# Cached value pages in even and odd partitions, with the score matmuls reading their keys in the same order

## The chip, the cores and the metric

The kernel runs on one core of one Trainium2 chip. The metric is the device time of one execution in microseconds (us), as the median of several runs. Beside it stands one execution taken by the hardware profiler, whose page and trace are read below.

## What is computed

One inference step of a hybrid decoder layer, for a prompt of 256 tokens and for eight sample sequences of eight new tokens each. The layer adds to its input, one after the other, a mixer (block attention beside a state-space scan), a cross-attention to a memory, and a squared-ReLU MLP. The change touches only the sample sequences' attention to their cached past of 1024 keys, which lie in eight pages of 128 keys; a page table names the pages. In the reference:

```
k_past = cache_k[l][page_table].reshape(bs, -1, ATT_HEADS, HEAD_DIM)
v_past = cache_v[l][page_table].reshape(bs, -1, ATT_HEADS, HEAD_DIM)
...
s = jnp.einsum('bhqd,bhqnkd->bhqnk', qq, kg)
s = jnp.where(mask, s, -jnp.inf).reshape(b, h, qc, n_sel * BLOCK)
p = jax.nn.softmax(s, axis=-1).reshape(b, h, qc, n_sel, BLOCK)
return jnp.einsum('bhqnk,bhqnkd->bhqd', p, vg)
```

A block is 256 keys, so two pages. Three of the four past blocks are attended to, chosen by the product of the query with the mean of the block's keys. Within a block the sum over keys, the maximum and the mean do not depend on the order of the keys, as long as scores and values have the same one.

## The kernel before

All weights are loaded in chunks of 128x1024 (512 KB, tile `wr`), each split by ScalarE and VectorE into a high and a low part (`wh` at L394, `wl` at L395). Each product of activations with weights is then three matmuls of type fp32r (L400, L401, L402). Attention works in plain f32, for which each matmul of the program stands in the trace as two instructions.

The order of TensorE's work is written out by hand as a string of letters, one for each piece of a stream; the letter `S` is the sample attention. The orders of ScalarE, VectorE, GpSimd and of the DMAs are lists of numbers. The change leaves all of them as they are.

`sample_attn(bp)` handles sequences 2bp and 2bp+1, for bp from 0 to 3. For each of the four blocks `n` it fetches, with `pages`, one tile `kv` of shape [128, 2, 512] for each sequence `e`: two pages, 256 KB each, by one DMA each on SyncE's queue (L841). Thirteen buffers of this size are shared by all that uses the name `kv`.

- Keys (`ckT`): a page is stored transposed, so that a partition is a component of the heads and the 512 columns are four groups of 128 keys. The score matmul (L882) takes as its moving operand `kbs[e][:, :, 128*c : 128*c+128]`, that is 128 neighbouring columns of the first page and then 128 of the second, 256 in all. Its stationary operand is the 32 columns of `qs`. Four such matmuls, for two sequences `e` and two groups of heads `g`, write four strips of 32 partitions of the PSUM tile `sc`. Each is done for s = 0 and 1.
- VectorE takes sums and maxima over the 256 columns (L885, L886), ScalarE the exponentials (L908), and TensorE transposes the result in pieces of 128 columns (L921), so that a piece's column becomes a partition of `pT`.
- Values (`cv`): partition k of page q holds the 512 values of key k in `t[:, q, :]`, a row of 2 KB. The value matmul (L936) for q = 0 contracts the first piece of 128 with the first page, that for q = 1 the second piece with the second page.

So a row of a `cv` transfer is 2 KB, and column 128*q + k of the scores is key k of page q.

Of the kernel before, what the change touches and what calls it, by code (L numbers as in the profile page):

```python
# [16 lines left out]
P = 128  # L17
# [105 lines left out]
def _constants():  # L123
    c = np.zeros((P, NCST), np.float32)
    i = np.arange(P)

    def put(name, a):
        lo, hi = CST[name]
        c[:, lo:hi] = a

    put("ident", np.eye(P))
    put("tri", i[:, None] <= i[None, :])
    put("gt", i[:, None] > i[None, :])
    diag = np.where(i[None, :] <= i[:, None], 0.0, NEG)
    put("cmask", np.concatenate([diag, np.zeros((P, P)), diag], axis=1))
    bq, tq = i // 64, i % 8

    om = np.full((P, 14, TS), NEG)
    for b in range(2):
        for t in range(TS):  # L140
            om[(bq == b) & (t <= tq), 6 + b, t] = 0.0
    put("omask", om.reshape(P, 112))
    s = np.arange(64)
    same = s[:, None] // TS == s[None, :] // TS
    a = np.zeros((P, 64))
    a[:64] = same & (s[:, None] <= s[None, :])
    put("tri_s", a)
    a = np.zeros((P, 64))
    a[:64] = same & (s[:, None] > s[None, :])
    put("gt_s", np.concatenate([a, a], axis=1))  # L150
    a = np.zeros((P, NB))
    a[:64] = s[:, None] // TS == np.arange(NB)[None, :]
    put("bmask", a)

    r = i // 32
    put("bquad", np.stack([i % 64 // TS == 4 * (r % 2) + 2 * e + r // 2 for e in range(2)], axis=1))
    put("selq", i[:, None] // 32 == np.arange(32)[None, :])
    put("sel0", np.arange(32)[None, :] == 0)
    put("sel4", np.arange(32)[None, :] == 4)
    put("idx", np.arange(1, 5)[None, :])  # L160
    put("ones", 1.0)
    half = np.float32(10000.0) ** (-np.arange(32, dtype=np.float32) / np.float32(32))
    pos = np.concatenate([np.arange(TP), np.tile(1024 + np.arange(TS), NB)]).astype(np.float32)
    ang = (pos[None, :] * half[:, None]).astype(np.float32)
    cos, sin = np.cos(ang), np.sin(ang)
    r = np.concatenate([np.tile(cos, (4, 1)), np.tile(sin, (4, 1))], axis=1)
    return c, r.astype(np.float32)
# [6 lines left out]
def _rows(w):  # L174

    k, m = w.shape
    return w.reshape(k // P, P, m // P, P).transpose(2, 1, 0, 3)


def _layout(a):  # L180
    f = {k: np.asarray(v) for k, v in a.items()}
    tok = np.concatenate([f["x_prompt"].reshape(TP, 1024), f["x_sample"].reshape(NB * TS, 1024)])
    o = {}
    o["xT"] = tok.T.reshape(8, P, T).transpose(1, 0, 2)
    o["memT"] = f["mem_prompt"].reshape(256, 1024).T.reshape(8, P, 256).transpose(1, 0, 2)
    wi = f["w_in"][0]

    def two(w):

        return _rows(w).reshape(4, 2, P, 512).transpose(0, 2, 1, 3)  # L190
    parts = [
        _rows(wi[:, HALF]), _rows(wi[:, 512 + HALF]), _rows(wi[:, 2048:3072]),
        wi[:, 1024:1536].reshape(4, 2, P, 512).transpose(0, 2, 1, 3), _rows(wi[:, 1536:2048]),
        two(f["w_out"][0][:512]), two(f["w_out"][0][512:]), _rows(f["wk_x"][0]), _rows(f["wq_x"][0]),
        f["wv_x"][0].reshape(4, 2, P, 512).transpose(0, 2, 1, 3),
        two(f["wo_x"][0]),
        _rows(f["w_up"][0]),
        _rows(f["w_down"][0]).reshape(8, P, 4, 1024).transpose(0, 2, 1, 3),
    ]
    o["w"] = np.concatenate([p.reshape(-1, P, 1024) for p in parts])  # L200
    npool = f["cache_k"].shape[1]
    o["ckT"] = f["cache_k"][0].reshape(npool, P, 512)[:, :, HALF].transpose(0, 2, 1).reshape(npool, 4, P, P).transpose(0, 2, 1, 3).reshape(npool, P, 512)
    o["cv"] = f["cache_v"][0].reshape(npool, P, 512)
    o["pt"] = f["page_table"].reshape(1, NB * NPAGE)
    o["mk"] = f["cache_mem_k"][0].transpose(0, 3, 2, 1).reshape(NB, P, 1024)
    o["mv"] = f["cache_mem_v"][0].reshape(NB, 2, P, 512).transpose(0, 2, 1, 3).reshape(NB, P, 1024)
    o["h0"] = f["state_ssm"][0].transpose(0, 3, 1, 2).reshape(NB, P, 512)
    o["sc"] = f["state_conv"][0].transpose(2, 0, 1).reshape(8, P, NB, 3).transpose(1, 0, 2, 3).reshape(P, 192)
    p = np.empty((P, NPRM), np.float32)

    def put(name, v):
        lo, hi = PRM[name]
        p[:, lo:hi] = v

    def cols(v):
        return v.reshape(-1, P).T

    put("g_mix", cols(f["ln_mix_g"]))
    put("g_x", cols(f["ln_x_g"]))
    put("g_mem", cols(f["ln_mem_g"]))  # L220
    put("g_mlp", cols(f["ln_mlp_g"]))
    put("g_ssm", cols(f["ssm_norm_g"]))
    put("conv_w", f["conv_w"][0].T.reshape(8, P, 4).transpose(1, 0, 2).reshape(P, 32))
    put("conv_b", cols(f["conv_b"]))
    put("d_skip", cols(np.repeat(f["d_skip"][0], 64)))
    for n, s in (("qg", f["q_norm_g"][0]), ("kg", f["k_norm_g"][0])):
        put(n, np.tile(s.reshape(2, 32), (1, 4)).T)
    put("qxg", f["qx_norm_g"][0][:, None])
    put("kxg", f["kx_norm_g"][0][:, None])
    put("dt_bias", np.broadcast_to(f["dt_bias"], (P, 8)))  # L230
    put("a_log", np.broadcast_to(f["a_log"], (P, 8)))
    put("w_dt", wi[:, 3072:3080].reshape(8, P, 8).transpose(1, 0, 2).reshape(P, 64))
    o["prm"] = p
    o["cst"], o["rot"] = _constants()
    return {k: np.ascontiguousarray(v) for k, v in o.items()}
# [22 lines left out]
def _body(tc, nc, I, O):  # L258
    V, A, G, S, PE = nc.vector, nc.scalar, nc.gpsimd, nc.sync, nc.tensor
# [40 lines left out]
    def ts(n=512):  # L300
        return tl(tp_, [P, n], "ts", bufs=NTS)
# [7 lines left out]
    def kv(shape, dt=F32):  # L309
        return tl(p1, list(shape), "kv", dt, bufs=NKV)  # L310
# [517 lines left out]
    def pages(b):  # L828

        with ExitStack() as st:  # L830
            if last_page:
                st.enter_context(tc.issue_after(last_page[-1]))
            _, idx = nc.values_load_multi_w_load_instructions(
                pt[0:1, NPAGE * b:NPAGE * b + NPAGE], engines=[mybir.EngineType.SP], min_val=0,
                max_val=I["ckT"].shape[0] - 1,
                skip_runtime_bounds_check_because="the page table indexes the pool")

        def get(name, n):
            t = kv([P, 2, 512])
            for q in range(2):  # L840
                d = S.dma_start(t[:, q, :], I[name][bass.ds(idx[2 * n + q], 1)].rearrange("o p c -> p (o c)"))  # L841
                last_page.append(d.ins)
            return t
        return get

    def sample_attn(bp):
# [29 lines left out]
        for n in range(4):  # L876
            kbs = [gets[e]("ckT", n) for e in range(2)]
            for s in range(2):
                for e in range(2):
                    for g in range(2):  # L880
                        r = 64 * e + 32 * g
                        PE.matmul(ps[r:r + 32, 256 * n:256 * n + 256], qs[:, s, g, b0 + e, :],  # L882
                                  kbs[e][:, :, 128 * (2 * g + s):128 * (2 * g + s) + 128], start=s == 0, stop=s == 1)
            if n % 2:
                V.reduce_sum(gs[:, n - 1:n + 1], pv[:, n - 1:n + 1, :], axis=AX.X)  # L885
                V.reduce_max(m5[:, n - 1:n + 1], pv[:, n - 1:n + 1, :], axis=AX.X)  # L886
            if n < 3:
                yield 1.05, PACE
# [41 lines left out]
        for n in range(4):  # L930
            vbs = [gets[e]("cv", n) for e in range(2)]
            for q in range(2):
                for e in range(2):
                    for g in range(2):
                        r = 64 * e + 32 * g
                        PE.matmul(yv[r:r + 32, 0:256], pT[:, 2 * n + q, r:r + 32], vbs[e][:, q, 256 * g:256 * g + 256],  # L936
                                  start=n == 0 and q == 0, stop=first and n == 3 and q == 1)
# [5 lines left out]
        if first:  # L943
# [21 lines left out]
            t = ts(256)  # L965
# [10 lines left out]
        for h in range(2):  # L976
            a = slice(64 * h, 64 * h + 64)
            for c in range(2):

                i0 = tp[a, 128 * c:128 * c + 128].rearrange("p (e g r) -> p g e r", e=2, g=2)[:, :, :, 16 * c + 8 * h:16 * c + 8 * h + 8]  # L980
                o = ay[a, c:4:2, TP + 16 * bp:TP + 16 * bp + 16].rearrange("p g (e t) -> p g e t", e=2)
# [4 lines left out]
    cv = xT  # L986
# [676 lines left out]
    def all_of(name, *gens):  # L1663
# [8 lines left out]
        return [one(g) for g in gens]  # L1672

    att = all_of("att", then(*[sample_attn(bp) for bp in range(4)]), then(prompt_attn(0), prompt_attn(1)))
    crs = all_of("cross", cross_sample(0), cross_prompt(0), cross_sample(1), cross_prompt(1))
    ys = all_of("y", ssd_all(), ssd_rest())
# [100 lines left out]
```

## Time and profile before

| what | value |
|---|---|
| median of 3 runs | 506.55 us (506.18 to 507.35) |
| the profiled execution's own time | 506.26 us |
| its span, first to last instruction | 504.5 us |
| TensorE busy | 497.7 us, 99% of the span |
| VectorE, ScalarE, GpSimd busy | 329.8, 264.2, 18.8 us |
| score matmuls (L882) | 256 instructions, 16.8 us of TensorE |
| value matmuls (L936) | 256 instructions, 15.4 us of TensorE |
| key and value pages | 64 transfers of 256 KB each |
| granted TensorE clock | 0.999 |

The span runs from the first to the last instruction; 1.8 us of the execution's time lie outside it. Busy time of a group is the union of its instructions, which can overlap on TensorE: each matmul is pipelined and its end is modelled. An engine's "idle before" is time in which it had nothing to run, with what ended it. The chain is followed backward from the last instruction to whatever released it.

### The profile page before, as it was taken

The numbers are of one execution on the slowest core, as the hardware profiler recorded it, in microseconds if no ns is written. First come the engines' busy times: TensorE is split into PE (matmuls) and PEld (weight loads), VectorE is DVE, ScalarE is ACT, GpSimd is POOL, SyncE is SP. The second block draws the span as 40 slices with busy tenths as digits, with TensorE's granted clock in tenths as the row PEclk, the third lists the DMA queues.
The fourth block names the chain that finished last, engine by engine and source line by source line (L and its number), as shares of the span: only waits on it lengthen the run. The fifth ranks groups of instructions, "written<-read, shape, count | busy, mean of one in ns | idle before, by whom it ended". The sixth has DMA issues, their size and how long they took to land.

```text
span 504.5 us, 10435 instructions
## 1 busy us (share of the span) xinstructions
PE 497.7 (99%) x3954; PEld 453.0 (90%) x3954; DVE 329.8 (65%) x681; ACT 264.2 (52%) x552; POOL 18.8 (4%) x58
## 2 busy tenths in 40 slices
PE   8999999999999999999999999999999999999997
PEld 5988787878676899998799999999999999999997
DVE  5878899687596898766659576875675443343431
ACT  7634447959766855646566564444455323233230
POOL 2400000130200000000000000000000000000000
PEclk9999999999999999999999999999999999999999
DMA  8999999899899257778903386553654644454530
GB/s 300 332 378 373 338 359 350 312 356 388 296 369 384 84 179 234 281 264 284 338 3 126 126 295 206 167 191 108 246 173 126 182 160 168 139 191 147 159 110 13
DMA packets 45508, 116.53 MB, mean 231 GB/s; under 512 B 5074, under 2 KB 7378, under 8 KB 45458
## 3 DMA queue, kind: packets, MB, share of 16 engines
q1 hardware_dynamic: 39122, 94.12, 54.1%
q10 hardware_dynamic: 6336, 21.75, 12.4%
q8 instruction: 31, 0.51, 0.4%
q14 instruction: 19, 0.16, 0.1%
HBM read 109.71 MB, written 6.14 MB: 230 GB/s over the span
## 4 chain that ended last, share of the span: by engine, by line
PE 94%; ACT 2%; DVE 2%; DMA 1%; issue 0%; SPq 0%; DVEq 0%
PE mm L400 24%; PE mm L401 23%; PE mm L402 23%; PE sc L882 3%; PE as L936 3%; PE ms L378 2%; PE sc L720 2%; PE as L378 1%; DMA wr<-w 1%; PE sc L1556 1%; PE ms L1658 1%; PE as L1580 1%; PE sc L1557 1%; PE mm L1630 1%; PE sc L1558 1%; PE as L1604 1%
## 5 line engine op out<-in xcount | busy, mean ns | idle before, releaser
L394 ACT ACTIVATE wh<-wr 128x1024 fp32r<-128x1024 f32 (+1 forms) x115 | 118.6, 1034 | 130.4 <-PE mm L401 104.7
L395 DVE TENSOR_TENSOR wl<-wr,wh 128x1024 fp32r<-128x1024 f32 (+1 forms) x115 | 137.0, 1195 | 74.6 <-ACT wh L394 73.6
L400 PE MATMUL mm<-big,wh 128*128 128x320 f32 x528 | 167.0, 316 | 0.0
L401 PE MATMUL mm<-big,wh 128*128 128x320 f32 x528 | 163.1, 309 | 0.1
L402 PE MATMUL mm<-big,wl 128*128 128x320 f32 x528 | 163.1, 309 | 0.0
L400 PEld LDWEIGHTS mm<-big,wh 128*128 128x128 f32 x528 | 99.1, 188 | 8.4 <-issue 6.0
L401 PEld LDWEIGHTS mm<-big,wh 128*128 128x128 f32 x528 | 99.2, 188 | 0.8 <-DVE big L1290 0.3
L402 PEld LDWEIGHTS mm<-big,wl 128*128 128x128 f32 x528 | 99.1, 188 | 0.0
L402 PE MATMUL mm<-hh,wl 128*128 128x320 f32 x256 | 78.9, 308 | 0.0
L401 PE MATMUL mm<-hl,wh 128*128 128x320 f32 x256 | 78.9, 308 | 0.0
L400 PE MATMUL mm<-hh,wh 128*128 128x320 f32 x256 | 78.9, 308 | 0.0
L401 PEld LDWEIGHTS mm<-hl,wh 128*128 128x128 f32 x256 | 48.1, 188 | 0.0
L400 PEld LDWEIGHTS mm<-hh,wh 128*128 128x128 f32 x256 | 48.1, 188 | 0.0
L402 PEld LDWEIGHTS mm<-hh,wl 128*128 128x128 f32 x256 | 48.1, 188 | 0.0
L1696 ACT ACTIVATE t<-t 128x320 f32<-128x320 f32 x32 | 14.5, 463 | 24.8 <-DVE t L1693 24.8
L1693 DVE SCALAR_TENSOR_TENSOR t<-mm,rb 128x320 f32<-128x320 f32 x30 | 14.6, 489 | 17.0 <-PE mm L402 13.6
L1697 DVE TENSOR_TENSOR hl<-t,hh 128x320 fp32r<-128x320 f32 x32 | 15.2, 487 | 5.8 <-ACT hh L1694 3.8
L1694 ACT ACTIVATE hh<-t 128x320 fp32r<-128x320 f32 x32 | 14.1, 458 | 8.1 <-DVE t L1693 8.1
L882 PE MATMUL sc<-kv,qs 128*32 128x256 f32 x256 | 16.8, 382 | 0.1
L1740 DVE TENSOR_TENSOR x2T<-mm,x2T 128x320 f32<-128x320 f32 (+1 forms) x9 | 4.0, 450 | 19.5 <-PE mm L402 19.5
L936 PE MATMUL as<-kv,p 128*32 128x256 f32 x256 | 15.4, 382 | 0.4 <-ACT p L922 0.4
L1009 DVE SCALAR_TENSOR_TENSOR t<-t,cwh,t 128x320 f32<-128x320 f32 x24 | 13.1, 547 | 3.2 <-ACT t L1007 1.4
(375 smaller groups left out, 643.5 us busy)
## 6 DMA issues: line engine op xcount, KB each, us to landing
wr<-w SPq DMA_DIRECT2D x69, 512.0 KB, 3.7
wr<-w ACTq DMA_DIRECT2D x41, 512.0 KB, 5.3
kv<-ckT SPq DMA_DIRECT2D x64, 256.0 KB, 5.3
kv<-cv SPq DMA_DIRECT2D x64, 256.0 KB, 6.0
kv<-mk SPq DMA_DIRECT2D x8, 512.0 KB, 4.2
kv<-mv SPq DMA_DIRECT2D x8, 512.0 KB, 6.5
kv<-h SPq DMA_DIRECT2D x4, 512.0 KB, 7.3
big<-h SPq DMA_DIRECT2D x4, 512.0 KB, 6.2
```

What stands on the lines that cost most here:

```text
L378: PE.transpose(out, in_, ident[:n, :n])
L394: A.activation(hi[:, c], raw[:, c], AF.Copy)
L395: V.tensor_tensor(lo[:, c], raw[:, c], hi[:, c], op=ALU.subtract)
L400: PE.matmul(out, hi[:, cols], xh, start=start, stop=False)
L401: PE.matmul(out, hi[:, cols], xl, start=False, stop=False)
L402: PE.matmul(out, lo[:, cols], xh, start=False, stop=stop)
L882: PE.matmul(ps[r:r + 32, 256 * n:256 * n + 256], qs[:, s, g, b0 + e, :], kbs[e][:, :, 128 * (2 * g + s):128 * (2 * g + s) + 128], start=s ...
L936: PE.matmul(yv[r:r + 32, 0:256], pT[:, 2 * n + q, r:r + 32], vbs[e][:, q, 256 * g:256 * g + 256], start=n == 0 and q == 0, stop=first and ...
L1693: V.scalar_tensor_tensor(t, ps[:, :T], 0.0, mlp["rb"], op0=ALU.max, op1=ALU.mult)
L1694: A.activation(hh[:, m, :], t, AF.Square)
L1696: A.activation(f, t, AF.Square)
L1697: V.tensor_tensor(hl[:, m, :], f, hh[:, m, :], op=ALU.subtract)
```

## The change

A pair's value pages are stored in another way. The two halves of a page's 128 keys are put side by side, so that row k of a page holds key k and then key 64 + k: 64 rows of 4 KB in place of 128 rows of 2 KB. The first page of a pair is written to the even partitions of the tile, the second to the odd ones. Partition 2k + q of `t[:, j, :]` is then key 64j + k of page q.

The scores have to take the keys in that order. The score matmul's moving operand, from the same key tile as before, goes through j (0, 1), then k (0 to 63), and innermost through the two pages q. Neighbouring columns of the operand are thus 512 floats, 2 KB, apart in the partition, where they were one float apart. Column 128*j + 2*k + q of the scores is key 64j + k of page q, and after the transpose its partition is 2k + q. The value matmul is written as before; its index q now stands for j.

```diff
-    o["cv"] = f["cache_v"][0].reshape(npool, P, 512)
+    o["cv"] = f["cache_v"][0].reshape(npool, 2, 64, 512).transpose(0, 2, 1, 3).reshape(npool, 64, 1024)
...
             for q in range(2):
-                d = S.dma_start(t[:, q, :], I[name][bass.ds(idx[2 * n + q], 1)].rearrange("o p c -> p (o c)"))
+                to = t[q:P:2].rearrange("p a c -> p (a c)") if name == "cv" else t[:, q, :]
+                d = S.dma_start(to, I[name][bass.ds(idx[2 * n + q], 1)].rearrange("o p c -> p (o c)"))
...
                         PE.matmul(ps[r:r + 32, 256 * n:256 * n + 256], qs[:, s, g, b0 + e, :],
-                                  kbs[e][:, :, 128 * (2 * g + s):128 * (2 * g + s) + 128], start=s == 0, stop=s == 1)
+                                  kbs[e][:, :, 128 * (2 * g + s):128 * (2 * g + s) + 128].rearrange("p q (j k) -> p j k q", j=2), start=s == 0, stop=s == 1)
```

No instruction changes its place on any engine; the line added in `get` shifts the lines after it by one. Two things move with the layout: the shape of the value transfers, and the waits of the value matmuls.

On SyncE's queue, the first value pages of the second pair (`kv_1477` is sequence 2's tile, `kv_1480` sequence 3's), before:

```order
L698 DMA out_kT<-kT_173 128x1280 [waits DMAHW4_49,DVE_49]
L841 ISA
L841 DMA kv_1477<-cv 128x512 [waits DMAHW5_49,PE_49]
L841 ISA
L841 DMA kv_1477<-cv 128x512 [waits DMAHW6_49]
```

and now:

```order
L698 DMA out_kT<-kT_173 128x1280 [waits DMAHW4_49,DVE_49]
L842 ISA
L842 DMA kv_1477<-cv 64x1024 [waits DMAHW5_49,PE_49]
L842 ISA
L842 DMA kv_1477<-cv 64x1024 [waits DMAHW6_49]
```

The place and the waits are the same, the shape is 64 rows of 1024 floats.

On TensorE, the value matmuls that read these tiles (`p_1341` is the transposed exponentials, `as_1476` the PSUM tile), before:

```order
L936 MATMUL as_1476<-kv_1477,p_1341 32x256 [waits DMAHW5_49,Activation_49]
L936 MATMUL as_1476<-kv_1477,p_1341 32x256
L936 MATMUL as_1476<-kv_1480,p_1341 32x256 [waits DMAHW0_49]
L936 MATMUL as_1476<-kv_1480,p_1341 32x256
L936 MATMUL as_1476<-kv_1477,p_1341 32x256 [waits DMAHW6_49]
L936 MATMUL as_1476<-kv_1477,p_1341 32x256
L936 MATMUL as_1476<-kv_1480,p_1341 32x256 [waits DMAHW1_49]
L936 MATMUL as_1476<-kv_1480,p_1341 32x256
```

and now:

```order
L937 MATMUL as_1476<-kv_1477,p_1341 32x256 [waits DMAHW6_49,DMAHW5_49,Activation_49]
L937 MATMUL as_1476<-kv_1477,p_1341 32x256
L937 MATMUL as_1476<-kv_1480,p_1341 32x256 [waits DMAHW1_49,DMAHW0_49]
L937 MATMUL as_1476<-kv_1480,p_1341 32x256
L937 MATMUL as_1476<-kv_1477,p_1341 32x256 x2
L937 MATMUL as_1476<-kv_1480,p_1341 32x256 x2
```

The wait for the second page of a tile has moved from the fifth and seventh matmul to the first and third, since each matmul now reads partitions of both pages.

## The prediction

> **What bounds the kernel now.** I read the page's busy times first, then the chain, then the two groups that the change touches, then TensorE's waits, and last the DMA rows.
>
> ```profile
> span 504.5 us, 10435 instructions
> PE 497.7 (99%) x3954; PEld 453.0 (90%) x3954; DVE 329.8 (65%) x681; ACT 264.2 (52%) x552; POOL 18.8 (4%) x58
> ...
> PE 94%; ACT 2%; DVE 2%; DMA 1%; issue 0%; SPq 0%; DVEq 0%
> ...
> L882 PE MATMUL sc<-kv,qs 128*32 128x256 f32 x256 | 16.8, 382 | 0.1
> ...
> L936 PE MATMUL as<-kv,p 128*32 128x256 f32 x256 | 15.4, 382 | 0.4 <-ACT p L922 0.4
> ```
>
> TensorE is busy for 497.7 of 504.5 us and makes up 94% of the chain; DMA has 1% of it. So a microsecond added to a matmul group is a microsecond of the result, while one taken from a transfer is worth something only where TensorE waits for that transfer. The list of TensorE's waits, all seven rows of it, of which the first two and the last stand here:
>
> ```profile
> PE ms L548 <- POOL ts L545: 1.4, 1, 1.4
> PE ms L378 <- ACT s L519: 0.6, 1, 0.6
> ...
> PE ms L378 <- PE as L936: 0.2, 1, 0.2
> ```
>
> No row names a DMA; the seven add up to 3.3 us, and the longest is the start. The transfers themselves are busy while pages move. These are the stretches in which the four pairs' values are fetched (length, then TensorE busy, its clock, DMA share, GB/s):
>
> ```profile
> 36.00:60.00 24.00, 23.76 (x203) 20.15 (x196) 18.56 (x52) 10.63 (x23) 0.26 (x2) 1.00 1.00 363
> 72.00:93.00 21.00, 20.97 (x219) 17.43 (x218) 19.91 (x50) 16.37 (x48) 1.48 (x8) 1.00 0.96 355
> 104.00:121.00 17.00, 17.00 (x193) 13.39 (x194) 14.64 (x40) 11.72 (x34) 2.96 (x12) 1.00 1.03 381
> 137.00:154.00 17.00, 17.00 (x183) 12.53 (x180) 14.84 (x37) 12.28 (x39) 0.63 (x2) 1.00 0.99 359
> ```
>
> The DMA engines are full (0.96 to 1.03), yet TensorE loses 0.24 us of 24 in the first stretch and nothing that shows in the last two. What covers the pages is the lead with which they are fetched. The last pair's keys and values, issue (SPq) and use (PE), and the landing times of all pages, shortest, median, longest:
>
> ```profile
> 134.96 0.85 SPq L841 DMA_DIRECT2D kv<-ckT  x2
> ...
> 145.22 1.07 PE L882 MATMUL sc<-kv,qs 128*32 128x256 f32 x16
> ...
> 148.07 0.85 SPq L841 DMA_DIRECT2D kv<-cv  x2
> ...
> 160.67 1.07 PE L936 MATMUL as<-kv,p 128*32 128x256 f32 x16
> ...
> DMA to landing us min/median/max: 3.1/5.9/7.7
> ```
>
> The last value pages are issued by 148.92 us; even with the longest landing they are there at 156.6, 4.0 us before 160.67. At the median the lead is 5.8 us.
>
> **The change part by part.** *Value transfers.* 64 transfers of 128 rows of 2 KB become 64 of 64 rows of 4 KB, at the same places in SyncE's queue and with the same bytes. What a packet is worth, from the page (queue: packets, MB, share of 16 engines' span):
>
> ```profile
> q1 hardware_dynamic: 39122, 94.12, 54.1%
> q10 hardware_dynamic: 6336, 21.75, 12.4%
> ...
> kv<-cv SPq DMA_DIRECT2D x64, 256.0 KB, 6.0
> ```
>
> Queue q1 has packets of 2406 bytes on average, which take 54.1% x 504.5 x 16 / 39122 = 112 ns; q10 has 3433 bytes in 12.4% x 504.5 x 16 / 6336 = 158 ns. A straight line through the two gives 3 ns for a packet and 45 ns for a KB. The 4096 packets that go away would then save 4096 x 3 ns / 16 = 0.8 us of the DMA engines' time, spread over the four stretches. It is hidden: nothing on TensorE waits for these transfers. I count 0. The ends: a gain of at most what TensorE still loses in the first two stretches, 0.24 + 0.03 us, and a loss if the new shape moves more slowly, which the third rival prices. SyncE issues the same 64 transfers at 333 ns each; that it waits inside these stretches for earlier transfers, and not they for it, is seen in its own list (the first row is the issues themselves, shortest, median and longest in ns):
>
> ```profile
> L841 SPq DMA_DIRECT2D kv<-cv x64: 332/333/1369, 34.5 to 148.6; - x64
> ...
> SPq L841 <- DMA wr<-w: 19.0, 12, 2.8
> ...
> SPq L841 <- DMA kv<-cv: 4.9, 8, 1.9
> ```
>
> *Waits of the value matmuls.* The first matmul of a block now waits for both pages of the tile, and everything behind it on TensorE with it. Before, the second page had some 0.4 us more, half of the 1.07 us of 16 instructions. With a lead of 4.0 us or more for the last pages, the wait has ended long before: 0. Without that cover it would cost at most 0.4 us x 16 blocks = 6.4 us.
>
> *Score matmuls.* This is the term that decides. Count, stationary operand, columns and order stay; only the steps of the moving operand change, from 4 bytes to 2 KB between neighbours. No row of the trace has a matmul that reads its moving operand with a step. So I bound it from the contiguous ones (start, length):
>
> ```profile
> 49.44 0.31 PE L400 MATMUL mm<-big,wh 128*128 128x320 f32 x1
> 49.59 0.31 PE L401 MATMUL mm<-big,wh 128*128 128x320 f32 x1
> ...
> 52.83 1.91 PE L882 MATMUL sc<-kv,qs 128*32 128x256 f32 x32
> ...
> 168.33 0.40 PE L1557 MATMUL sc<-wl,kv 128*128 128x512 f32 x1
> 168.56 0.40 PE L1558 MATMUL sc<-wh,kv 128*128 128x512 f32 x1
> ...
> 245.72 1.99 PE L1630 MATMUL mm<-kv,qz 128*128 128x256 f32 x8
> ```
>
> An fp32r matmul of 512 columns starts 0.23 us after the one before: 0.45 ns a column. Eight plain f32 matmuls of the whole array (L1630, 386 ns each) take 1.99 us, so they start (1.99 - 0.386) / 7 = 0.229 us apart: 0.89 ns a column. And 32 score instructions take 1.91 us; if four strips run side by side, that is 8 steps of (1.91 - 0.38) / 7 = 0.219 us, 0.86 ns a column. They must run side by side, since four in a row at L1630's 0.229 us would need 0.92 us. Two things follow. A plain f32 instruction takes a column only every 0.86 ns, 1.9 times as long as the array's input has been seen to need in fp32r. And the four strips, each with columns of its own, are fed at once at no loss.
>
> So if a jump at every column halves the rate of each strip's input, the input still gives a column in 2 x 0.45 = 0.90 ns, and a step of four takes 0.230 us in place of 0.219: 64 steps x 0.011 = 0.7 us. If it costs less, it costs nothing. If the four strips share what fetches the columns, and neighbours that lie together were fetched together, the price is larger: a doubled step is 64 x 0.219 = 14.0 us, a quadrupled one (each of four strips' columns fetched in turn) 42 us. All of it would lie on the path, since TensorE has 99%. Below zero there is nothing, since the arithmetic sets the pace. I take 0, the end nearest to the row of the score matmuls: plain f32 leaves the input almost twice the time it has been seen to need.
>
> The Trainium skill speaks against this choice (SBUF — State Buffer, Door 1: The DMA port swizzle, its note on cachelines): "consecutive accesses to the same 16-byte line hit full bandwidth", and each access that crosses to another line pays a penalty. Here every column crosses. The page gives no size for TensorE; halving would be the 0.7 us above.
>
> *Everything after the scores* (sums, maxima, exponentials, transposes, value matmuls) has the same shapes and works on contiguous columns: 0.
>
> *Sum.* 506.26 us of the profiled execution (504.5 span and 1.8 around it) + 0 - 0 = 506.3. The median of the runs lies 0.3 us above that execution, so 506.5 us for a median.
>
> **The rivals.** *1. Strided columns slow the scores: slower.* For it: no contiguous row excludes it, and four strips together take 4 x 256 columns in 0.219 us, 4.7 a ns, far more than the 2.2 of one fp32r stream, so what feeds them may well lean on neighbours being together. Against it: the slack of 1.9 per strip. It decides once a step exceeds 0.219 + 1.0 / 64 = 0.235 us. Doubled, the likeliest of its sizes: 506.5 + 14 = 520.5 us. Quadrupled: 548. By the skill's rule on lines, this is the rival that comes true, with a size that the page leaves open.
>
> *2. Faster pages gain something.* The DMA engines are full for about 79 us, and 0.8 us of their time is freed. Against it stands that TensorE waits for no DMA; the gain is bounded by the idle 0.27 us above, and with an earlier weight chunk here and there perhaps 1.2 us: 505.3 us.
>
> *3. The 64-row transfers are slower: slower too.* Sixteen value transfers of a pair are 4.2 MB, 11.6 us at 363 GB/s. At half the rate they take 11.6 us more while the engines are full, and the lead absorbs 4.0: up to 7.6 us for each of four pairs, 30 us in all, 537 us; a third slower (3.9 us) is absorbed. It decides from there. For it: full DMA engines, and no load of 64 rows in the trace. Against it: q10 and q1 move a byte at the same speed whatever the packet.
>
> The skill's page on SBUF (same section) says that a transfer to partitions 0 to 63 reaches only half of the ports and measures 196 GB/s for 128 partitions' 328. By the formula there, even or odd partitions alone reach all ports, so the rule as such does not strike here; no run shows it yet.
>
> **How the numbers follow.** 0.2%, 1.0 us, is about what a measurement of this kernel can tell from no change. No change in the scores' pace and pages hidden: 0.57. Rival 1: 0.28, of which 0.05 just over the bound (507.5 to 510), 0.16 near the doubled step, 0.07 beyond. Rival 3: 0.10, half of it below 521. Rival 2: 0.05. So faster 0.05, same 0.57, slower 0.38. The likeliest case alone would lie within 505.6 to 507.5 us. To hold 8 in 10 the range must take in the doubled step: 505.4 to 521.5 us holds 0.57 + 0.21 + 0.05 and part of rival 2, and leaves out the quadrupled step and the heavy transfers.
>
> **What would show it.** In the profile after, the score matmuls' line (L883 there) would have 256 instructions at 379 to 382 ns and 16.8 us busy, and 32 of them would take 1.91 us; a slow input shows there first, as 30 us busy for a doubled step. The DMA packets would fall by 4096 from 45508. The value pages would land in about 6 us, and no DMA would stand in the list of TensorE's waits. The value matmuls' line would stay at 15.4 us. Wrong would be the prediction if the score line's busy time grows by more than 1 us, or if TensorE idles before the value matmuls for a page.

## The result, and the profile after

| | before | after |
|---|---|---|
| median, same chip (6 runs each) | 506.69 us | 509.15 us |
| ratio, 95% interval | | 1.0051 (1.0041 to 1.0061) |
| profiled span | 504.5 us | 507.1 us |

The change makes the kernel 2.5 us slower. The forecast was 506.5 us, no change. The page of the kernel after, with the rows that answer to those shown of before (the lines behind the changed one are numbered one higher, so the scores are L883 and the value matmuls L937):

```profile
span 507.1 us, 10463 instructions
PE 500.8 (99%) x3954; PEld 454.5 (90%) x3954; DVE 329.6 (65%) x681; ACT 264.7 (52%) x552; POOL 18.5 (4%) x58
...
DMA packets 41412, 116.53 MB, mean 230 GB/s; under 512 B 5074, under 2 KB 7378, under 8 KB 41362
...
q1 hardware_dynamic: 35026, 94.12, 53.5%
...
PE 97%; ACT 2%; DVE 1%; issue 0%; POOL 0%; DVEq 0%; POOLq 0%
...
L883 PE MATMUL sc<-kv,qs 128*32 128x256 f32 x256 | 20.4, 438 | 0.0
...
L937 PE MATMUL as<-kv,p 128*32 128x256 f32 x256 | 15.5, 382 | 0.4 <-ACT p L923 0.4
...
kv<-cv SPq DMA_DIRECT2D x64, 256.0 KB, 6.0
```

One group has grown: the score matmuls are busy for 20.4 us, where they had 16.8, and one takes 438 ns in place of 382. The other signs that the prediction named stand as it said: 4096 packets fewer, value pages landing in 6.0 us, value matmuls at 15.5 us. The timeline (start, length) shows the same 32 score instructions that took 1.91 us before, and the last pair's value pages and their use:

```profile
53.06 2.35 PE L883 MATMUL sc<-kv,qs 128*32 128x256 f32 x32
...
151.01 1.14 SPq L842 DMA_DIRECT2D kv<-cv  x2
...
163.31 1.07 PE L937 MATMUL as<-kv,p 128*32 128x256 f32 x16
```

(2.35 - 0.434) / 7 = 0.274 us for a step of four strips; the starts of the instructions themselves stand 0.271 us apart, where they stood 0.216 apart before. Over 64 steps that is 64 x 0.055 = 3.5 us. TensorE's busy time grows by 3.1 us, the span by 2.6. Not all of the 3.5 us arrives: from the start of the first score matmul to the end of the last, 100.0 us become 102.9. Part of the rest went into waits that were there anyway. A transpose (L378) that waited for ScalarE started 0.34 us behind the matmul ahead of it (90.24 and 90.58 us); it now starts 0.15 us behind (91.86 and 92.01 us). The stretch ahead of the first score is 0.2 us shorter in this execution, which the change cannot have caused, and the one behind the last score takes 358.2 us in both.

One thing has moved that the prediction took as fixed: SyncE needs 475 ns (median) to issue a value transfer, where it needed 333. The last row is the landing time of all pages, keys and values:

```profile
L842 SPq DMA_DIRECT2D kv<-cv x64: 474/475/1375, 35.1 to 151.7; - x64
...
DMA to landing us min/median/max: 3.3/5.8/8.3
```

TensorE's list of waits still names no DMA; these are its first and its last row of six:

```profile
PE ms L548 <- POOL ts L545: 1.4, 1, 1.4
...
PE ms L378 <- PE as L937: 0.2, 1, 0.2
```

### The profile page after: what moved, and what is told of

Same layout as the page of the kernel before. It is cut to its first block, busy times and chain, and to the rows that moved or that the text cites. A ratio compares the mean times of both kernels' runs of the same rounds, so it can differ in the third digit from the quotient of the medians.

```text
span 507.1 us, 10463 instructions
## 1 busy us (share of the span) xinstructions
PE 500.8 (99%) x3954; PEld 454.5 (90%) x3954; DVE 329.6 (65%) x681; ACT 264.7 (52%) x552; POOL 18.5 (4%) x58
## 4 chain that ended last, share of the span: by engine, by line
PE 97%; ACT 2%; DVE 1%; issue 0%; POOL 0%; DVEq 0%; POOLq 0%
PE mm L400 24%; PE mm L401 23%; PE mm L402 23%; PE sc L883 4%; PE as L937 3%; PE ms L378 2%; PE sc L720 2%; PE as L378 1%; PE ms L548 1%; PE sc L1557 1%; PE ms L1659 1%; PE as L1581 1%; PE sc L1558 1%; PE mm L1631 1%; PE sc L1559 1%; PE as L1605 1%
## 5 line engine op out<-in xcount | busy, mean ns | idle before, releaser
L883 PE MATMUL sc<-kv,qs 128*32 128x256 f32 x256 | 20.4, 438 | 0.0
L937 PE MATMUL as<-kv,p 128*32 128x256 f32 x256 | 15.5, 382 | 0.4 <-ACT p L923 0.4
L883 PEld LDWEIGHTS sc<-kv,qs 128*32 128x32 f32 x256 | 8.5, 110 | 7.4 <-issue 1.3
```

## Experiments

In all but x3_step4, x4_halves and the two probes, some of the sample sequences' attention is computed with values of other keys, as each expectation says. The two probes take 62 and 47 us longer by the work that they add behind the end; only the added instructions are read from them. The others were run beside the kernel before, whose median there was 506.48 us (x1, x2, x4) and 506.43 us (x5, x3).

### Each half of the change alone

The theory from the comparison of the two traces: the loss is all in the pace of the score matmuls, as in the prediction's first rival. Its rivals: the value transfers' new shape, or the waits that moved, take a share. `x1_scores` is the kernel before with the score edit alone:

```diff
-    kbs[e][:, :, 128 * (2 * g + s):128 * (2 * g + s) + 128], ...
+    kbs[e][:, :, 128 * (2 * g + s):128 * (2 * g + s) + 128].rearrange("p q (j k) -> p j k q", j=2), ...
```

> Only the scores' column order of the change; the value pages are fetched as before, so each weight meets another key's values. If the slower score matmuls are the whole cause, a score instruction takes 434 ns (before 379), the group is busy for 20.4 us, and the time is 2.5 us above the kernel before, as the change's is. If part of the loss comes from the value transfers or from the waits that were moved to the first value matmuls, it is less, 1.5 us or below.

`x2_values` is the kernel after with the score operand of before, so with the new transfers and the moved waits alone:

```diff
-    kbs[e][:, :, 128 * (2 * g + s):128 * (2 * g + s) + 128].rearrange("p q (j k) -> p j k q", j=2), ...
+    kbs[e][:, :, 128 * (2 * g + s):128 * (2 * g + s) + 128], ...
```

> Only the value pages of the change, 64 rows of 4 KB in even or odd partitions; the scores go through the keys as before, so each weight meets another key's values. If the score matmuls are the whole cause: within 0.3 us of the kernel before, score instructions at 379 ns, 4096 packets fewer. If the moved waits cost something (28 more wait instructions stand in the change's trace, 51 ns each): up to 1.4 us slower. If the shape of the transfers cost something: value pages land clearly later than 6.0 us.

Measured: x1_scores 509.2 us, ratio to before 1.0058 (1.0044 to 1.0071); x2_values 506.44 us, ratio 1.000 (0.9991 to 1.0009). The score group's row, from the trace of x1_scores and then from that of x2_values:

```profile
L882 PE MATMUL sc<-kv,qs 128*32 128x256 f32 x256 | 20.4, 438 | 0.0
```

```profile
L883 PE MATMUL sc<-kv,qs 128*32 128x256 f32 x256 | 16.9, 382 | 0.1
```

The scores alone cost 2.7 us, which is all of the change's loss; the transfers and the waits cost nothing that can be measured. The 28 added wait instructions and the longer issue of the value transfers (475 ns here too) are hidden, or below 0.5 us. The 4096 packets saved bring nothing either. Whether they free any time of the DMA engines does not show: queue q1 is busy for 272.9 us before (54.1% of 504.5), for 272.2 us in x2_values (53.9% of 505.0), but for 273.9 us in x5_runs4 (54.2% of 505.4), a run shown below with the same value transfers. This scatter is larger than the 0.8 us that the prediction estimated.

### What it is in the operand that costs: a probe of ten patterns

Two theories of why. "Turns": each new beginning of the pattern's innermost loop costs 0.42 ns; the change has 128 of them per matmul, which makes 54 ns. "Lines": a column that is not a neighbour of the one before costs 0.21 ns; 256 of them make 54 ns too. `p1_probe` adds matmuls behind the end, over a tile that lies there already (`hf`, 10240 floats in a partition), for each pattern `view`:

```diff
+    for letter, view in looks:
+        o = bank("one" + letter)
+        for _ in range(4):
+            PE.matmul(o[:, 0:256], ident, moving(0, view).bitcast(F32), start=True, stop=True)
+        o = bank("four" + letter)
+        for _ in range(4):
+            for r in range(4):
+                PE.matmul(o[32 * r:32 * r + 32, 0:256], ident[:, 32 * r:32 * r + 32], moving(2048 * r, view).bitcast(F32), start=True, stop=True)
+        o = bank("fast" + letter)
+        for _ in range(8):
+            PE.matmul(o[:, 0:256], hl[:, 0, 0:128], moving(0, view), start=True, stop=True)
```

> The kernel before with matmuls of 256 columns added behind its end (their results are not used), over ten patterns of the moving operand, each as plain f32 on the whole array, as plain f32 in four strips, and as fp32r. Theory turns: each new beginning of the innermost loop costs 0.42 ns, whatever its step. Theory lines: each column that does not lie beside its neighbour costs 0.21 ns in plain f32. Longer step between instructions of one strip than for contiguous columns, turns / lines, in ns: two runs of 128: 0 / 0. Pairs 512 apart, as in the change: 54 / 54. Step of 2 floats in one loop: 0 / 27 or less. Step of 4 floats in one loop: 0 / 54. Inner loop of 4, 256 apart: 27 / 54. Inner loop of 16, 64 apart: 7 / 54. Runs of 2 alternating between two places: 54 / 27 or 0. Runs of 4: 27 / 13 or 0. Runs of 16: 7 / 3 or 0. A third possibility, that only four strips at once suffer: nothing on the whole array, 54 in four strips. In fp32r, turns says the same ns as in plain f32; lines says at least double the step, 0.9 ns a column.

Measured, as the median distance in ns between the starts of consecutive instructions (of consecutive steps of four strips):

| pattern of 256 columns | plain f32, whole array | plain f32, four strips | fp32r |
|---|---|---|---|
| contiguous (c) | 216 | 216 | 118 |
| two runs of 128, as before (b) | 216 | 216 | 120 |
| to and fro, 512 apart, as after (q) | 271 | 271 | 112 |
| step of 2 floats (d) | 227 | 227 | 230 |
| step of 4 floats (e) | 453 | 453 | 233 |
| four places, 256 apart (g) | 438 | 439 | 143 |
| sixteen places, 64 apart (h) | 433 | 667 | 277 |
| runs of 2, alternating between two places (i) | 227 | 227 | 166 |
| runs of 4 (j) | 216 | 216 | 129 |
| runs of 16 (k) | 216 | 216 | 120 |

The groups of some of these patterns in the probe's trace. The tile's name begins with `one` for the whole array, `four` for four strips and `fast` for fp32r, and ends with the letter of the table (mean ns of an instruction behind the comma; it lies some 160 to 190 above the distance of the starts):

```profile
L1768 PE MATMUL foure<-hh,cst 128*32 128x256 f32 x32 | 3.8, 629 | 0.0
L1764 PE MATMUL onee<-hh,cst 128*128 128x256 f32 x8 | 3.8, 632 | 0.0
...
L1768 PE MATMUL fourq<-hh,cst 128*32 128x256 f32 x32 | 2.4, 437 | 0.0
L1764 PE MATMUL oneq<-hh,cst 128*128 128x256 f32 x8 | 2.3, 434 | 0.0
...
L1771 PE MATMUL faste<-hh,hl 128*128 128x256 f32 x8 | 2.1, 424 | 0.0
L1771 PE MATMUL fastd<-hh,hl 128*128 128x256 f32 x8 | 2.1, 419 | 0.0
...
L1764 PE MATMUL onei<-hh,cst 128*128 128x256 f32 x8 | 2.0, 393 | 0.0
...
L1764 PE MATMUL onej<-hh,cst 128*128 128x256 f32 x8 | 1.9, 380 | 0.0
...
L1764 PE MATMUL onec<-hh,cst 128*128 128x256 f32 x8 | 1.9, 379 | 0.0
...
L1771 PE MATMUL fastc<-hh,hl 128*128 128x256 f32 x8 | 1.2, 293 | 0.0
...
L1771 PE MATMUL fastq<-hh,hl 128*128 128x256 f32 x8 | 1.2, 288 | 0.0
```

Neither theory holds as it stood. Turns falls: a step of 4 floats has one loop and no turns, and costs 237 ns; runs of 4 have 64 turns and cost nothing. Lines has the direction right and the size wrong: single columns 4 floats apart double the matmul's time, and going to and fro between two places costs only 55 of these 237 ns. The third possibility falls too: one operand on the whole array is slowed exactly as four strips are, except with sixteen places. And what is slow in plain f32 is not what is slow in fp32r: there, to and fro is free and a step of 2 costs as much as a step of 4.

### Does the distance matter?

The theory after the probe: neighbouring floats are fetched together and kept for a while, so that a place that comes back soon costs less ("places"). Its rival: the cost depends on how far apart the two places are, and another distance, by padding the tile, would be free ("distance"). `p2_places` adds patterns in the same way, with distances D in `m[:, 0:2*D].rearrange("p (q k) -> p k q", q=2)[:, 0:128, :]`, and a few more.

> The kernel before with matmuls of 256 columns added behind its end (results not used), plain f32 and fp32r on the whole array. Theory places: neighbouring floats are fetched together and kept for a while; going to and fro between two places costs some 55 ns whatever their distance, four places cost as much as single columns, a step of 8 floats as much as 4. Theory distance: the cost hangs on how far apart the places are, so that among distances of 128, 132, 144, 256, 516, 528, 1024 and 4096 floats some cost nothing in plain f32. In ns over 216: places: 55 for all eight distances, about 220 for four places at 512 or 516, 237 for a step of 8; and for two of every four neighbouring floats 11 or less. Distance: 0 for 132, 144, 516 and 528 and 55 for the others, or the like, and four places 516 apart cost clearly less than 512 apart.

Measured in the same way, plain f32 on the whole array, then fp32r: for D of 128, 132, 144, 256, 512 (q above), 516, 528, 1024 and 4096 floats 270 to 271 ns each, and 112 each. Three places 291 ns (252 columns; not tried in fp32r). Four places 512 or 516 apart: 438 and 440; 143 and 137. Two of every four neighbouring floats: 227; 227. Step of 3: 340; 234. Step of 8: 460; 218. The nearest and the farthest pair of places, from the groups of this trace:

```profile
L1767 PE MATMUL onea<-hh,cst 128*128 128x256 f32 x8 | 2.3, 434 | 0.0
...
L1767 PE MATMUL oneh<-hh,cst 128*128 128x256 f32 x8 | 2.3, 435 | 0.0
```

Distance falls: nine distances, one price. Places holds in plain f32, in all that it gave numbers for. Steps of 1, 2, 3, 4 and 8 cost 216, 227, 340, 453 and 460 ns. If 4 floats are fetched at once, these 256 columns need 64, 128, 192, 256 and 256 fetches. 227/128, 340/192 and 453/256 are each 1.77 ns, and 460/256 is 1.80; 64 fetches at that price would be done in 113 ns, well within 216. So, by this estimate, a fetch costs 1.77 ns in plain f32, and the time rises once fewer than 2 columns are used of each. Runs of 2 from two places fit as well (128 fetches, 227 ns).

One thing that the estimate leaves open is the change's own pattern. To and fro between two places would cost 453 ns if every column needed a fetch of its own, and 216 if what is fetched were kept until it is used up. It costs 271, so it is kept in part; why just so much, and why four places cost almost the full price (438), is not shown.

The Trainium skill's note on cachelines (SBUF — State Buffer, Door 1: The DMA port swizzle) has this rule: lines of 16 bytes, and at least two hits on a line for full bandwidth. In plain f32 the probe agrees within 5%: two columns of a line 227 ns, where contiguous ones take 216, and one 453. In fp32r it does not: two columns of a line cost 227 to 230 ns, about the 233 of one, against 118 for contiguous ones.

### The change with runs of four keys

If the single columns are the cause, then the whole change with four keys of a page at a time should lose nothing. `x5_runs4`:

```diff
-    ... .rearrange("p q (j k) -> p j k q", j=2), ...
+    ... .rearrange("p q (k i) -> p k q i", i=4), ...
```

> The whole change, but the scores take four neighbouring keys of the first page, then four of the second, in place of one and one; values stay as in the change, so each weight meets another key's values. If the pace of the score operand is the whole loss and single columns from alternating places are what slows it: score instructions at 379 ns, 16.8 us for the group, and the time of the kernel before within 0.5 us. If the loss came from anything else in the change, or from reading two places in turn at all: 508 us or more.

Measured: 506.33 us, ratio to before 1.000 (0.9991 to 1.0009). Its score group:

```profile
L883 PE MATMUL sc<-kv,qs 128*32 128x256 f32 x256 | 16.8, 382 | 0.1
```

Two places read in turn cost nothing when four neighbours are taken each time. The rest of the change is there and is free.

This run settles the cause, but it is no finished kernel. For its scores to meet their own values, a page would have to lie in groups of four partitions (0 to 3, 8 to 11 and so on, the other page in between). No run here has such transfers, and `x4_halves`, below, shows that the choice of 64 partitions can cost more than the scores do.

### A dearer operand in its place

To see that the price goes through to the end, `x3_step4` gives the scores an operand with one column in four, by another layout of the key pages:

```diff
-    ... .reshape(npool, 4, P, P).transpose(0, 2, 1, 3).reshape(npool, P, 512)
+    ... .reshape(npool, 4, P, P).transpose(0, 2, 3, 1).reshape(npool, P, 512)
...
-    kbs[e][:, :, 128 * (2 * g + s):128 * (2 * g + s) + 128], ...
+    kbs[e][:, :, 2 * g + s::4], ...
```

> The kernel before, with the four groups of a key page interleaved, so that the score operand's 256 columns lie 4 floats apart, in one loop; keys and values in the order of before. By the added matmuls of the probe (453 ns a step in place of 216): score instructions at about 616 to 632 ns, the group 64 x 0.237 = 15 us longer, and the time 14 us above before, since TensorE sets it. If the longer matmuls found cover beside waits that are there anyway: clearly less, below 10 us. The theory of turns, which the probe speaks against, says no change.

Measured: 521.14 us, ratio 1.0288 (1.0272 to 1.0303), so 14.7 us above before. Its score group:

```profile
L882 PE MATMUL sc<-kv,qs 128*32 128x256 f32 x256 | 32.0, 631 | 0.0
```

15.2 us more of TensorE, of which 14.7 reach the end. The prediction's "doubled step", priced at 14.0 us, is this operand and not the one of the change.

### The pages in halves

The loss could also be avoided by giving the first page partitions 0 to 63 and the second 64 to 127: the rows stay 4 KB, and the scores go through four runs of 64 neighbouring keys. `x4_halves`, against the kernel after, with keys and values matched:

```diff
-                to = t[q:P:2].rearrange("p a c -> p (a c)") if name == "cv" else t[:, q, :]
+                to = t[64 * q:64 * q + 64].rearrange("p a c -> p (a c)") if name == "cv" else t[:, q, :]
...
-    ... .rearrange("p q (j k) -> p j k q", j=2), ...
+    ... .rearrange("p q (j k) -> p j q k", j=2), ...
```

> The first page of a pair in partitions 0 to 63 and the second in 64 to 127, still 64 rows of 4 KB; the scores then go through j, q and k, in four runs of 64 neighbouring columns. If the loss comes from beginning a short inner loop 128 times, or from columns that lie apart: score instructions at 379 to 381 ns and the time of the kernel before, within 0.4 us. If 64 neighbouring partitions are a slower place to write than 64 alternate ones: value pages at half the rate land at 9 us or later where DMA is full, and the kernel is slower than the change, by up to 30 us.

Measured: 528.32 us, ratio 1.0429 (1.0409 to 1.0449): 21.8 us slower than before. The score matmuls are at their old pace; the value pages land in 9.0 us (median), where they took 6.0. Its score group, its value transfers, and the stretches of 72 to 93 and 104 to 121 us (last two numbers: DMA share, GB/s):

```profile
L883 PE MATMUL sc<-kv,qs 128*32 128x256 f32 x256 | 16.8, 382 | 0.1
...
kv<-cv SPq DMA_DIRECT2D x64, 256.0 KB, 9.0
...
72.00:93.00 21.00, 19.68 (x221) 15.96 (x220) 19.21 (x54) 12.94 (x34) 0.96 (x5) 1.00 1.04 312
104.00:121.00 17.00, 12.96 (x171) 8.16 (x170) 10.17 (x19) 9.12 (x21) 3.86 (x12) 0.90 1.05 320
```

The same DMA engines are as busy as before and move less: 312 and 320 GB/s where the kernel before had 355 and 381. TensorE idles for 4 of 17 us in the second stretch. It hardly waits for the pages themselves, 0.3 us in the whole execution:

```profile
PE as L378 <- ACT yn L972: 4.0, 1, 4.0
...
PE as L937 <- DMA kv<-cv: 0.3, 1, 0.3
```

The chain in the second stretch shows how the delay comes to it:

```profile
97.01 10.12 DMA kv<-cv
107.13 0.02 issue
107.15 0.33 ACTq L342
107.49 0.05 issue
107.53 0.48 ACT t L1012
...
114.07 0.47 ACT yn L972
114.53 0.04 issue
114.58 0.69 PE as L378 x2
```

ScalarE's instructions include the issue of weight loads (L342). One of them waits for a value transfer that takes 10.1 us, and everything behind it on ScalarE waits with it. TensorE then waits for ScalarE: its next transpose (L378) needs `yn`.

Waits are not all of it. Against the trace before, TensorE's idle time grows by 16.5 us (6.8 to 23.3) and its busy time by 6.8 us (497.7 to 504.5). Part of the longer busy time is a lower clock: the granted clock of the second stretch is 0.90, against 1.00 before. It is 0.5 in three pieces of 3.4 us, which begin at 114.1, 138.0 and 148.2 us and in which TensorE is busy for 8.8 us together; at full clock that would be 4.4 us less, by estimate.

The Trainium skill's section on the port swizzle (SBUF — State Buffer, Door 1: The DMA port swizzle), named in the prediction, says that partitions 0 to 63 reach half of the ports, and its formula gives all ports to alternate partitions. No run here counts ports, but the times agree with both: 64 alternate partitions cost nothing (x2_values, landing in 5.8 us), 64 neighbouring ones land in 9.0 us, in a kernel that is 21.8 us slower.

No version here beats the kernel before: the 4 KB rows bring nothing that TensorE would notice, so the best of them only lose nothing.

## Why the prediction was wrong

- **The score matmuls: this step failed.** The prediction took 0 for the strided operand, between ends of 0 and 42 us, since "plain f32 leaves the input almost twice the time it has been seen to need". It measured 55 ns a step, 3.5 us of TensorE, 2.7 us at the end (x1_scores). What failed is that the input's pace was carried over from fp32r to plain f32. The prediction's price of a jump, 0.90 ns a column, is about what separate columns take in fp32r (233/256 = 0.91 ns). In plain f32 they take twice that (453/256 = 1.77 ns), and the change's to and fro takes 271/256 = 1.06 ns, where the prediction saw room up to 0.86. And the very pattern that costs 55 ns in plain f32 is free in fp32r.
- **The direction of the first rival was right and its size off.** "The four strips share what fetches the columns" is not what happens: one operand on the whole array pays the same. The real size, 2.5 us, lay in the part "just over the bound (507.5 to 510)", to which the prediction gave 0.05 of its 0.28, while it gave 0.16 to a doubled step. That the stated range of 505.4 to 521.5 us holds the result is luck: it reaches so far for the doubled step, which did not occur.
- **That the path carries it: right in the main.** Of 3.5 us added to TensorE 2.5 to 2.7 reached the end, of 15.2 us 14.7. Between the first and the last score, 0.6 to 0.8 us went into waits that were there and into overlap.
- **Value transfers at 0: right**, by x2_values. Whether 0.8 us of DMA time are freed, the traces cannot tell, since queue q1 differs by more between runs. That SyncE issues them at 333 ns each was wrong (475), and hidden.
- **Moved waits at 0: right**; the trace after has no DMA in TensorE's list of waits. The last pages are issued by 152.15 us and need 8.3 us at most, which is 2.9 us ahead of their use at 163.31.
- **The third rival** did not come true for the change. Something like it exists: with neighbouring partitions in place of alternate ones the pages do move more slowly, and the kernel loses 21.8 us, of the 30 that the prediction gave as a bound. But the path is another: TensorE waits for ScalarE, which stands behind a transfer, and part is the lower clock.

## What to carry to other kernels

Before an operand of a matmul is rearranged for a transfer's sake, look at how many neighbouring floats it still takes at a time: in plain f32 four or more cost nothing here, two 5%, one from two alternating places 25%, and one alone doubles the matmul. On a kernel that TensorE bounds and whose pages arrive early, larger DMA rows have nothing to give, so any price on TensorE is a loss. If 64 partitions are written by one transfer, alternate ones were as good as 128 here, and neighbouring ones slowed all that shares the DMA engines.

## What was not expected of the hardware

- Plain f32 and fp32r matmuls react differently to the same operand: to and fro between two places 271 against 216 ns in plain f32, 112 against 118 in fp32r; a step of 2 floats 227 against 216, but 230 against 118.
- With sixteen places in turn, four strips at once are slower (667 ns) than one operand on the whole array (433); no other pattern showed such a difference in the median step. Why, and what in the fetch makes plain f32 and fp32r differ, these runs do not settle.
- The distance between two places does not matter, from 128 to 4096 floats.
- SyncE takes longer to issue 64 rows of 4 KB than 128 rows of 2 KB: 475 ns (469 for neighbouring partitions) against 333.
